# Two token mixers, each with its own order and priorities of parts

## The chip, the core and the metric

The program runs on one core of a Trainium2 chip. The metric is the device time of one execution in microseconds, as a median over runs. The engines are named as the profile names them: PE (TensorE, matrix products; PEld is its weight load), DVE (VectorE), ACT (ScalarE), POOL (GpSimd) and SP (SyncE, which here only issues transfers).

## The reference, cut to what matters

Two layers work on 256 tokens of 1024 features, in float32:

```
x = x + 0.5 * swiglu(rms_norm(x), ...)               # first half step
proj = rms_norm(x) @ w_in                            # RWKV | attention | gates
o_a = rwkv7_mixer(...)      # two scans (forward, backward), 8 heads of 64
o_b = diff_attention(...)   # 4 heads, two softmax maps each
x = x + (sigmoid(g_A) * (o_a @ P_A) + sigmoid(g_B) * (o_b @ P_B)) @ w_out
x = x + 0.5 * swiglu(rms_norm(x), ...)               # second half step
```

The scan multiplies a 64 x 64 state of each head by a decay, corrects it by a rank-one term and adds an outer product for every token. It is the part that can't be written as one large product.

## The kernel before, in words

Activations lie with features in partitions. A large product runs in three float32r passes over a split of both operands in a high and a low part. So a weight tile of 128 x 1024 goes through `weights` (L129): SP issues its load (`wr`, L133), ACT rounds it (`wh`, L135), DVE subtracts to get the rest (`wl`, L139), and PE multiplies (L145 to L147, 24 products of 256 columns for a tile of a projection; L643 to L645, 12 of 512 columns, for attention).

The scan is done in chunks of 64 tokens. Two heads make a pair, and there are four pairs. The parts of a mixer, by the names that the plan uses, are:

- `rw`: low-rank decay and rate parts (three projected tiles). `k0` to `k3`: key and receptance of a pair (two tiles each, `shifted`, L227, whose DVE step on the finished bank is L233). `v0`, `v1`: values of two pairs (two tiles each).
- `w0` to `w3`: a pair of heads (`pair_front`, `unit_front`, `unit_back`). `unit_back` multiplies into PSUM banks of the pool `back` (L331, L337), and DVE empties them under masks (L409, L410, L416, L418 or L421). The last `unit_back` of a pair is held until the next `rwkv_rest`; `x0` and `x1` call it for pairs 1 and 3.
- `i0`, `i1` (`invert`, L435): inverses of the 32 x 32 diagonal blocks of pairs 0, 1 and of pairs 2, 3. The blocks go through DRAM so that one lies in each partition, and then DVE does 22 products (L458) and 22 sums (L459), each of which needs the one before. The first are of a few elements, the last of 1024. POOL multiplies the blocks by a mask meanwhile (L452). The scratch `tv` has one buffer, so `i1` runs after `i0`.
- `m0`, `m1` (`merge_blocks`): the blocks off the diagonal. `c0`, `c1` (`chain`): the scan over four chunks for two pairs each; `c1` also does the group norms (last DVE step L607).
- `at`: twelve weight tiles of attention and the norms of queries and keys (L655 to L663). `ac`: attention itself, head by head; its last steps give `ob`, which shows as icl (L718, L719).
- `g1`, `g0`: eight gate tiles for each branch. `B`: the first branch's product, of `ob`. Behind the plan come branch A, the output product and the next half step.

What runs when is set by a planner at compile time. It simulates the program and hands out, on each engine, the instruction that is ready and comes first by number; the number is the place in the text, and `high_priority(n)` takes n places off it (a negative n adds places). So an instruction further back in the plan fills in where those before it aren't ready. `@` (`issue_after`) queues a part's PE instructions behind the last PE instruction of another part. Tiles of one tag are given out in the order of the text, whatever the numbers are: three places for `wr` and `wh`, two for `wl`, two each for the banks `gen` and `back`, one for `att`. The queue of each engine is fixed then, and the chip runs it in order.

Before, both layers use one string (L37) and one table of priorities (L40):

```
PLAN = "rw k0 w0 k1 w1 x0 i0 k2 w2 v0 k3 w3 v1@w1 x1 i1 m0 c0 m1 c1 at ac@w0 g1@k3 g0@m1 B@w2"
PR = {'k3': -150, 'B': 60}
```

Of the kernel before, what the change touches and what calls it, by code (L numbers as in the profile page):

```python
"""Hybrid bidirectional encoder trunk: macaron SwiGLU halves around RWKV-7 and differential attention.

Activations stay feature-major on chip ([feature in partition, feature tile, token]); weights stream
once. Float32 products of the large matrices are carried by float32r passes over an exact split of
both operands into a high and a low part.
"""
# [11 lines left out]
F32 = mybir.dt.float32  # L18
F32R = mybir.dt.float32r
AF = mybir.ActivationFunctionType  # L20
ALU = mybir.AluOpType
# [3 lines left out]
P = 128  # L25
# [11 lines left out]
PLAN = "rw k0 w0 k1 w1 x0 i0 k2 w2 v0 k3 w3 v1@w1 x1 i1 m0 c0 m1 c1 at ac@w0 g1@k3 g0@m1 B@w2"  # L37
T3 = 0
GATE = {}
PR = {'k3': -150, 'B': 60}  # L40
# [5 lines left out]
# tiles that share a place with others  # L46
PLACE = {"b0": "ar0", "b1": "ar1", "b2": "wt0", "b3": "wt1", "b4": "ab", "b5": "qb", "ak2": "x"}

# columns of the packed vectors
# [5 lines left out]
class Trunk:  # L55
# [21 lines left out]
    def slot(self, tag, shape, dt=F32, half=False):  # L77
        """A tile of 8 KB (or 4) in a partition; tiles of one tag follow each other in place."""
        tag, n = PLACE.get(tag, tag), int(np.prod(shape[1:]))
        t = self.sp.tile([P, 1024 if half else 2048], dt, tag=tag, name=self.nm(tag))  # L80
        v = t[:, :n]
        names = "abcd"[:len(shape) - 1]
        if len(names) > 1:
            v = v.rearrange(f"p ({' '.join(names)}) -> p {' '.join(names)}", **dict(zip(names, shape[1:])))
        return v
# [42 lines left out]
    # weights ------------------------------------------------------------------------------------  # L128
# [56 lines left out]
    # feed-forward half step ---------------------------------------------------------------------  # L185
# [32 lines left out]
    # one tile of x @ W for two feature tiles, in a bank -----------------------------------------  # L218
# [8 lines left out]
    def shifted(self, l, tiles, outs):  # L227
        """outs = p + mu * (centred_shift(p) - p) of RWKV column tiles."""
# [86 lines left out]
    def rwkv_pair(self, p):  # L315
        """A pair of heads in both directions; the last part of the second direction waits for the next call."""
# [16 lines left out]
    def turn(self, out, a):  # L333
        """out[h] = a[h].T for both halves of the partitions."""
# [25 lines left out]
    def unit_front(self, p, d, st, sig, a2, da):  # L360
# [3 lines left out]
        # 2 * iclr - 1 = tanh of half the logit  # L364
# [32 lines left out]
    def unit_back(self, p, d, st, bw, kw):  # L397
# [26 lines left out]
        if d == 1:  # L424
            # sum over a head of r * r_k * (k of both directions)
# [8 lines left out]
    # (I - A)^-1 of the 32 x 32 diagonal blocks, one in a partition ---------------------------------  # L434
    def invert(self, q):  # L435
# [25 lines left out]
        # 16 x 16 blocks, row by row from below: X[i, j:] = G[i, j:] X[j:, j:]  # L461
# [7 lines left out]
        # the block off the diagonal: X01 = X00 G01 X11, with X00 G01 in the place below G's diagonal  # L469
# [19 lines left out]
    def merge_blocks(self, q):  # L489
        """The blocks off the diagonal: T = D + D A D."""  # L490
# [17 lines left out]
    # the scans, chunk by chunk --------------------------------------------------------------------  # L508
    def chain(self, l, q):
        """Two pairs of heads, both directions: the forward scan at chunk j, the other at chunk 3 - j."""  # L510
# [98 lines left out]
    # differential attention -----------------------------------------------------------------------  # L609
# [19 lines left out]
    def attention(self, l):  # L629
        nc, io, vec = self.nc, self.io, self.vec[l]  # L630
        mm = nc.tensor.matmul
        qkt = self.qkt = self.slot("icl", [P, 2, 4, S])
        va = self.va = self.slot("va", [P, 2, 512], half=True)
        for i in range(3):
            ps = [self.acc(), self.acc()]
            for c in range(4):
                wh, wl = self.weights(io["watt"][l, i, :, c * CW:(c + 1) * CW], CW)
                for b in range(2):
                    k = 2 * c + b
                    h, w = wh[:, b * 512:(b + 1) * 512], wl[:, b * 512:(b + 1) * 512]  # L640
                    for t in range(2):
                        ts = slice(t * P, (t + 1) * P)
                        mm(ps[t], self.xh[:, k, ts], h, start=k == 0, stop=False)  # L643
                        mm(ps[t], self.xl[:, k, ts], h, start=False, stop=False)
                        mm(ps[t], self.xh[:, k, ts], w, start=False, stop=k == KD - 1)  # L645
            for t in range(2):
                sc = self.rsT[:, t:t + 1]
                if i == 2:
                    nc.scalar.activation(va[:, t], ps[t], AF.Copy, scale=sc)
                    continue  # L650
                q, sq = [self.f2().rearrange("p a (b c) -> p (a b) c", c=64) for _ in range(2)]
                nc.scalar.activation(q, ps[t].rearrange("p (a b) -> p a b", a=8), AF.Copy, scale=sc)
                nc.scalar.activation(sq, q, AF.Square)
                ms, rq = self.tmp("n8", [P, 8], bufs=4), self.tmp("n8", [P, 8], bufs=4)
                nc.vector.tensor_reduce(ms, sq, AX.X, ALU.add)  # L655
                nc.vector.tensor_scalar(ms, ms, 1.0 / 64, EPS, ALU.mult, ALU.add)
                nc.gpsimd.tensor_tensor(rq, ms, self.mhalf[:, 0:8], ALU.pow)
                nc.vector.tensor_tensor(q, q, rq.unsqueeze(2).to_broadcast([P, 8, 64]), ALU.mult)
                pt = self.att()
                qf = q.rearrange("p a b -> p (a b)")  # L660
                for h in range(4):
                    nc.tensor.transpose(pt[:, h * P:(h + 1) * P], qf[:, h * P:(h + 1) * P], self.ident)
                nc.scalar.activation(qkt[:, i, :, t * P:(t + 1) * P], pt.rearrange("p (a b) -> p a b", a=4), AF.Copy,  # L663
                                     scale=vec[:, V_QG + i:V_QG + i + 1])

    def attention_core(self, l):
# [3 lines left out]
        for h in range(4):  # L670
# [17 lines left out]
            # e0 / s0 - lambda * e1 / s1 = (e0 - lambda * s0 / s1 * e1) / s0  # L688
# [32 lines left out]
    # the token mixer ------------------------------------------------------------------------------  # L721
    def gates(self, l, b):
        """2 * sigmoid - 1 = tanh of half the logits, kept in DRAM until the branch is ready; a step a feature tile."""
# [197 lines left out]
```

## Time and profile before

| | |
|---|---|
| Median of three runs (lowest, highest) | 1406.25 us (1405.81, 1408.23) |
| Profiled execution, first to last instruction | 1406.5 us |
| PE busy | 1349.9 us (96%) |
| PEld busy | 1285.0 us (91%) |
| DVE busy | 940.7 us (67%) |
| ACT busy | 664.8 us (47%) |
| POOL busy | 288.2 us (20%) |

The page gives no other time of the profiled execution than its span, which is 0.3 us above the median of the runs. PE is busy nearly throughout, so what an order can change is the time in which PE waits. The half steps have next to none. The two mixers lie at about 217 to 515 us and 910 to 1210 us, and the slices of the page in which PE drops below its usual share are theirs.

### The profile page before, as it was taken

The numbers are of one execution on the slowest core, as the hardware profiler recorded it, in microseconds if no ns is written. First come the engines' busy times: TensorE is split into PE (matmuls) and PEld (weight loads), VectorE is DVE, ScalarE is ACT, GpSimd is POOL, SyncE is SP. The second block draws the span as 40 slices with busy tenths as digits, with TensorE's granted clock in tenths as the row PEclk, the third lists the DMA queues.
The fourth block names the chain that finished last, engine by engine and source line by source line (L and its number), as shares of the span: only waits on it lengthen the run. The fifth ranks groups of instructions, "written<-read, shape, count | busy, mean of one in ns | idle before, by whom it ended". The sixth has DMA issues, their size and how long they took to land.

```text
span 1406.5 us, 30996 instructions
## 1 busy us (share of the span) xinstructions
PE 1349.9 (96%) x12916; PEld 1285.0 (91%) x12916; DVE 940.7 (67%) x1421; ACT 664.8 (47%) x1059; POOL 288.2 (20%) x284
## 2 busy tenths in 40 slices
PE   6999999998989999999999999999988999999999
PEld 6999998877889899999999999988767888999998
DVE  4655557799957766555556655588999577656644
ACT  5444445344444455444444444554543554544432
POOL 3111015445001112111111111154540010211100
PEclk9999999999999999999999999999999999999999
DMA  6555664325333565556655556633352445555564
GB/s 230 182 181 182 180 207 156 99 91 138 108 103 116 191 229 177 185 181 179 181 184 187 183 174 183 218 111 113 93 143 83 114 136 193 175 187 184 183 188 143
DMA packets 90333, 227.60 MB, mean 162 GB/s; under 512 B 29264, under 2 KB 35408, under 8 KB 89680
## 3 DMA queue, kind: packets, MB, share of 16 engines
q1 hardware_dynamic: 78640, 207.16, 47.0%
q10 hardware_dynamic: 11552, 18.46, 3.9%
q8 instruction: 101, 1.65, 0.5%
q14 instruction: 40, 0.33, 0.1%
HBM read 214.05 MB, written 11.53 MB: 160 GB/s over the span
## 4 chain that ended last, share of the span: by engine, by line
PE 80%; DVE 11%; DMA 3%; issue 2%; ACT 2%; POOL 2%; ACTq 0%; SPq 0%; DVEq 0%; POOLq 0%
PE acc L147 23%; PE acc L146 23%; PE acc L145 23%; DVE tv L458 3%; DVE wl L139 3%; DVE lora L459 2%; PE back L331 1%; PE gen L331 1%; PE att L679 1%; PE back L337 1%; PE gen L283 1%; DMA x<-xd 1%; DMA x<-x 1%; DMA f<-g 0%; PE acc L643 0%
## 5 line engine op out<-in xcount | busy, mean ns | idle before, releaser
L135 ACT ACTIVATE wh<-wr 128x1024 fp32r<-128x1024 f32 (+1 forms) x390 | 404.9, 1039 | 414.7 <-PE acc L146 268.6
L139 DVE TENSOR_TENSOR wl<-wr,wh 128x1024 fp32r<-128x1024 f32 (+1 forms) x390 | 475.5, 1219 | 171.0 <-PE acc L147 83.0
L145 PE MATMUL acc<-xh,wh 128*128 128x256 f32 x1904 | 540.2, 286 | 11.8 <-ACT wh L135 11.8
L146 PE MATMUL acc<-xl,wh 128*128 128x256 f32 x1904 | 539.5, 285 | 0.0
L147 PE MATMUL acc<-xh,wl 128*128 128x256 f32 x1904 | 529.9, 286 | 2.4 <-DVE wl L139 2.1
L145 PEld LDWEIGHTS acc<-xh,wh 128*128 128x128 f32 x1904 | 367.0, 193 | 17.3 <-ACT wh L135 12.0
L146 PEld LDWEIGHTS acc<-xl,wh 128*128 128x128 f32 x1904 | 367.0, 193 | 3.2 <-issue 2.5
L147 PEld LDWEIGHTS acc<-xh,wl 128*128 128x128 f32 x1904 | 360.6, 193 | 9.4 <-issue 3.5
L204 POOL TENSOR_TENSOR t<-t,t 128x256 f32<-128x256 f32 x88 | 89.3, 1016 | 403.7 <-ACT t L202 403.7
L145 PE MATMUL acc<-ar,wh 128*128 128x256 f32 x512 | 144.9, 283 | 0.0
L147 PE MATMUL acc<-ar,wl 128*128 128x256 f32 x512 | 144.9, 283 | 0.0
L199 DVE TENSOR_TENSOR t<-acc,rs 128x512 f32<-128x512 f32 x88 | 60.8, 692 | 119.7 <-PE acc L147 114.6
L146 PE MATMUL acc<-wt,wh 128*128 128x256 f32 x384 | 108.9, 284 | 0.0
L145 PEld LDWEIGHTS acc<-ar,wh 128*128 128x128 f32 x512 | 98.3, 192 | 0.0
L147 PEld LDWEIGHTS acc<-ar,wl 128*128 128x128 f32 x512 | 98.3, 192 | 0.0
L145 PE MATMUL acc<-wt,wh 128*128 128x256 f32 x320 | 91.0, 286 | 3.4 <-DVE x L839 2.2
L166 POOL TENSOR_TENSOR vv<-vv,t 128x256 f32<-128x256 f32 x42 | 36.8, 876 | 279.4 <-ACT t L165 271.8
L147 PE MATMUL acc<-wt,wl 128*128 128x256 f32 x320 | 91.5, 286 | 1.3 <-DVE wl L139 1.2
L458 DVE TENSOR_TENSOR tv<-lora 64x8 f32<-64x8 f32 (+10 forms) x88 | 74.9, 852 | 1.9
L146 PEld LDWEIGHTS acc<-wt,wh 128*128 128x128 f32 x384 | 74.4, 194 | 0.0
L146 PE MATMUL acc<-ab,wh 128*128 128x256 f32 x256 | 72.4, 283 | 0.0
L145 PEld LDWEIGHTS acc<-wt,wh 128*128 128x128 f32 x320 | 61.9, 194 | 4.0 <-issue 2.4
(234 smaller groups left out, 1935.1 us busy)
## 6 DMA issues: line engine op xcount, KB each, us to landing
wr<-f1i SPq DMA_DIRECT2D x88, 512.0 KB, 3.7
wr<-f2i SPq DMA_DIRECT2D x88, 512.0 KB, 3.6
wr<-win SPq DMA_DIRECT2D x62, 512.0 KB, 3.6
wr<-f1o SPq DMA_DIRECT2D x32, 512.0 KB, 3.6
wr<-f2o SPq DMA_DIRECT2D x32, 512.0 KB, 3.6
wr<-watt SPq DMA_DIRECT2D x24, 512.0 KB, 3.7
wr<-wbr SPq DMA_DIRECT2D x16, 512.0 KB, 3.6
wr<-wout SPq DMA_DIRECT2D x16, 512.0 KB, 3.4
```

Source lines behind the costliest of these rows:

```text
L135: nc.scalar.activation(wh[:, :n], raw[:, :n], AF.Copy)
L139: nc.vector.tensor_tensor(wl[:, :n], raw[:, :n], wh[:, :n].bitcast(F32), ALU.subtract)
L145: mm(out, wh, xh, start=first, stop=False)
L146: mm(out, wh, xl, start=False, stop=False)
L147: mm(out, wl, xh, start=False, stop=last)
L166: nc.gpsimd.tensor_tensor(self.sq, self.sq, sq, ALU.add)
L199: nc.vector.tensor_tensor(gu, ps.rearrange("p (a b) -> p a b", a=2), self.rs.unsqueeze(1).to_broadcast([P, 2, S]), ALU.mult)
L204: nc.gpsimd.tensor_tensor(h, s, gu[:, 1], ALU.mult)
L283: mm(ps, dw[r, t * P:(t + 1) * P], w2[r], start=True, stop=True)
L331: self.nc.tensor.matmul(out[r], a[r], b[r], start=start, stop=stop)
L458: mul = lambda o, a, b: ops.append(nc.vector.tensor_tensor(o, a, b, ALU.mult).ins)
L459: add = lambda o, a: ops.append(nc.vector.tensor_reduce(o, a, AX.X, ALU.add).ins)
```

## The change

One plan and one table of priorities become two of each, chosen by the layer. In the first layer `i0` and `i1` come behind all four pairs (`k2 k3 w2 v0 w3 x1 i0 v1 i1`), `c1` comes behind `at` and `ac`, `B` loses its `@w2`, and `w0` and `v1` get numbers 150 places lower and `k2` 200 higher. The second layer keeps the old order; `w2` gets `@w0`, and `g0` and `c1` get numbers 300 and 100 places higher. `attention` and `gates` can be called in pieces now, but both plans call them whole (`at` loops over the three pieces in place).

```diff
-PLAN = "rw k0 w0 k1 w1 x0 i0 k2 w2 v0 k3 w3 v1@w1 x1 i1 m0 c0 m1 c1 at ac@w0 g1@k3 g0@m1 B@w2"
+PLANS = (
+    "rw k0 w0 k1 w1 x0 k2 k3 w2 v0 w3 x1 i0 v1@w1 i1 m0 c0 m1 at ac@w0 c1 g1@k3 g0@m1 B",
+    "rw k0 w0 k1 w1 x0 i0 k2 w2@w0 v0 k3 w3 v1@w1 x1 i1 m0 c0 m1 c1 at ac@w0 g1@k3 g0@m1 B@w2",
+)
...
-PR = {'k3': -150, 'B': 60}
+PRS = ({'k3': -150, 'B': 60, 'v1': 150, 'k2': -200, 'w0': 150},
+       {'k3': -150, 'B': 60, 'g0': -300, 'c1': -100})
...
-    def attention(self, l):
+    def attention(self, l, i):
...
         elif f == "at":
-            self.attention(l)
+            for i in range(3):
+                self.attention(l, i)
...
-        for f in PLAN.split():
+        for f in PLANS[l].split():
             f, *after = f.split("@")
...
-                with self.tc.high_priority(PR[f]) if PR.get(f) else nullcontext():
+                with self.tc.high_priority(PRS[l][f]) if PRS[l].get(f) else nullcontext():
                     self.part(l, f)
```

## Rows read from the trace of the kernel before

**Rows 1.** The page: its first line, and DVE's split of the weights.

```profile
span 1406.5 us, 30996 instructions
...
L139 DVE TENSOR_TENSOR wl<-wr,wh 128x1024 fp32r<-128x1024 f32 (+1 forms) x390 | 475.5, 1219 | 171.0 <-PE acc L147 83.0
```

**Rows 2.** Stretches of both mixers: length, busy time by engine, granted clock, DMA.

```profile
core 0: us, PE busy (x) PEld busy (x) DVE busy (x) ACT busy (x) POOL busy (x), PEclk, DMA share, GB/s
217.00:280.00 63.00, 62.61 (x624) 54.51 (x624) 50.53 (x92) 32.84 (x58) 33.61 (x37) 1.00 0.36 113
280.00:343.30 63.30, 57.95 (x529) 46.52 (x528) 61.72 (x119) 27.15 (x48) 32.84 (x23) 0.95 0.36 110
343.30:394.00 50.70, 44.45 (x569) 39.40 (x569) 47.97 (x74) 24.30 (x40) 0.62 (x1) 0.87 0.43 122
394.00:466.00 72.00, 68.61 (x1079) 62.35 (x1075) 46.67 (x99) 35.92 (x84) 6.83 (x8) 0.99 0.40 122
...
973.00:1040.00 67.00, 59.73 (x546) 47.82 (x544) 63.84 (x116) 30.11 (x50) 39.02 (x23) 0.97 0.38 114
```

**Rows 3.** Timeline of PE, 294 to 333 us: where it waited (start, us, idle before).

```profile
298.67 1.15 PE L337 MATMUL back<-ident,t 64*64 64x64 f32 x32 [1.55 <-DVE qb L410]
301.69 0.40 PE L331 MATMUL back<-ar,t 64*64 64x128 f32 x2 [1.41 <-DVE n L656]
...
327.80 1.15 PE L337 MATMUL back<-ident,t 64*64 64x64 f32 x32 [1.11 <-DVE n L656]
330.26 1.97 PE L331 MATMUL back<-ar,t 64*64 64x128 f32 x16 [1.19 <-DVE qk L418]
```

**Rows 4.** Timeline of DVE ahead of the first two waits.

```profile
296.60 0.74 DVE L458 TENSOR_TENSOR tv<-lora 64x338 f32<-64x338 f32 x1
...
297.79 0.41 DVE L409 TENSOR_TENSOR ab<-back,masks 128x256 f32<-128x256 f32 x1
298.12 0.41 DVE L410 TENSOR_TENSOR qb<-back,masks 128x256 f32<-128x256 f32 x1
...
301.14 0.41 DVE L418 TENSOR_TENSOR qk<-back,masks 128x256 f32<-128x256 f32 x1
```

**Rows 5.** Stretches, the inversions' products (L458) alone: length, DVE busy, clock, DMA.

```profile
280.00:343.30 63.30, 20.78 (x22) 0.95 0.36 110
343.30:391.00 47.70, 16.95 (x22) 0.90 0.43 123
```

**Rows 6.** The same stretches, the inversions' sums (L459) alone.

```profile
280.00:343.30 63.30, 11.60 (x22) 0.95 0.36 110
343.30:391.00 47.70, 11.20 (x22) 0.90 0.43 123
```

**Rows 7.** Timelines of DVE: largest product of each inversion, and the last sum.

```profile
337.17 4.25 DVE L458 TENSOR_TENSOR tv<-lora 64x1024 f32<-64x1024 f32 x1
...
387.03 1.88 DVE L458 TENSOR_TENSOR tv<-lora 64x1024 f32<-64x1024 f32 x1
...
389.40 1.22 DVE L459 TENSOR_REDUCE lora<-tv 64x64 f32<-64x1024 f32 x1
```

**Rows 8.** Timeline of POOL beside the first inversion.

```profile
312.40 0.74 POOL L385 TENSOR_TENSOR t<-t,kr 128x256 f32<-128x256 f32 x1 [4.06 <-ACT t L377]
314.93 4.59 POOL L384 TENSOR_TENSOR ar<-kr,e 128x256 f32<-128x256 f32 x1 [1.79 <-ACT e L375]
...
337.09 2.39 POOL L452 TENSOR_TENSOR ab<-ab,masks 128x1024 f32<-128x1024 f32 x1 [3.06 <-DMA d<-ab]
```

**Rows 9.** Timelines of PE and DVE at the first mixer's end: attention's and the scan's last.

```profile
465.37 0.62 PE L145 MATMUL acc<-icl,wh 128*128 128x256 f32 x3 [0.78 <-ACT icl L718]
...
479.30 0.42 DVE L607 TENSOR_TENSOR x<-t,x 128x256 fp32r<-128x256 f32 x1
```

**Rows 10.** Timeline of DVE: the last of the eight L233 steps of the first mixer.

```profile
281.76 0.67 DVE L233 TENSOR_TENSOR t<-acc,rs 128x512 f32<-128x512 f32 x1
```

**Rows 11.** Timeline of SP's queue: the last gate weights, the first of branch B.

```profile
427.28 7.31 SPq L133 DMA_DIRECT2D wr<-win  x2
440.69 0.33 SPq L133 DMA_DIRECT2D wr<-wbr  x1
```

More of the change, by code (lines that the diff above doesn't have):

```diff
@@ L627, in lambdas @@
         nc.vector.tensor_scalar(sg, vec[:, V_SG:V_SG + 1], 1.0 - lam_init, None, ALU.mult)
-    def attention(self, l):
+    def attention(self, l, i):
         nc, io, vec = self.nc, self.io, self.vec[l]
         mm = nc.tensor.matmul
[L632 to L664, printed above, removed]
@@ new lines, in attention @@
+        if self.qkt is None:
+            self.qkt = self.slot("icl", [P, 2, 4, S])
+            self.va = self.slot("va", [P, 2, 512], half=True)
+        qkt, va = self.qkt, self.va
+        ps = [self.acc(), self.acc()]
+        for c in range(4):
+            wh, wl = self.weights(io["watt"][l, i, :, c * CW:(c + 1) * CW], CW)
+            for b in range(2):
+                k = 2 * c + b
+                h, w = wh[:, b * 512:(b + 1) * 512], wl[:, b * 512:(b + 1) * 512]
+                for t in range(2):
+                    ts = slice(t * P, (t + 1) * P)
+                    mm(ps[t], self.xh[:, k, ts], h, start=k == 0, stop=False)
+                    mm(ps[t], self.xl[:, k, ts], h, start=False, stop=False)
+                    mm(ps[t], self.xh[:, k, ts], w, start=False, stop=k == KD - 1)
@@ new lines, in attention @@
+        for t in range(2):
+            sc = self.rsT[:, t:t + 1]
+            if i == 2:
+                nc.scalar.activation(va[:, t], ps[t], AF.Copy, scale=sc)
+                continue
+            q, sq = [self.f2().rearrange("p a (b c) -> p (a b) c", c=64) for _ in range(2)]
+            nc.scalar.activation(q, ps[t].rearrange("p (a b) -> p a b", a=8), AF.Copy, scale=sc)
+            nc.scalar.activation(sq, q, AF.Square)
+            ms, rq = self.tmp("n8", [P, 8], bufs=4), self.tmp("n8", [P, 8], bufs=4)
+            nc.vector.tensor_reduce(ms, sq, AX.X, ALU.add)
+            nc.vector.tensor_scalar(ms, ms, 1.0 / 64, EPS, ALU.mult, ALU.add)
+            nc.gpsimd.tensor_tensor(rq, ms, self.mhalf[:, 0:8], ALU.pow)
+            nc.vector.tensor_tensor(q, q, rq.unsqueeze(2).to_broadcast([P, 8, 64]), ALU.mult)
+            pt = self.att()
+            qf = q.rearrange("p a b -> p (a b)")
+            for h in range(4):
+                nc.tensor.transpose(pt[:, h * P:(h + 1) * P], qf[:, h * P:(h + 1) * P], self.ident)
+            nc.scalar.activation(qkt[:, i, :, t * P:(t + 1) * P], pt.rearrange("p (a b) -> p a b", a=4), AF.Copy,
+                                 scale=vec[:, V_QG + i:V_QG + i + 1])
@@ L719, in attention_core, with gates @@
             nc.vector.scalar_tensor_tensor(ob[:, 1, :, ts], p4, sg, ob[:, 0, :, ts].bitcast(F32), ALU.mult, ALU.subtract)
-    def gates(self, l, b):
+    def gates(self, l, b, tiles):
         nc = self.nc
-        gd = self.gd[b] = self.dp.tile([4, P, 2, S], F32, tag=f"g{b}", name=self.nm(f"g{b}"))
-        for j in range(KD):
+        if b not in self.gd:
+            self.gd[b] = self.dp.tile([4, P, 2, S], F32, tag=f"g{b}", name=self.nm(f"g{b}"))
+        gd = self.gd[b]
+        for j in tiles:
             ps = self.project(self.io["win"][l], [15 + 8 * b + j])
@@ L794, in part @@
         elif f == "at":
-            self.attention(l)
+            for i in range(3):
+                self.attention(l, i)
+        elif f in ("a0", "a1", "a2"):
+            self.attention(l, int(f[1]))
         elif f == "ac":
@@ L798, in part @@
         elif f[0] == "g":
-            for _ in self.gates(l, int(f[1])):
+            tiles = {"": range(8), "a": range(4), "b": range(4, 8)}[f[2:]]
+            for _ in self.gates(l, int(f[1]), tiles):
                 pass
@@ L810, in mix @@
         self.lambdas(l)
-        self.gd = {}
+        self.gd, self.qkt = {}, None
         marks = {}
-        for f in PLAN.split():
+        for f in PLANS[l].split():
             f, *after = f.split("@")
```

## The prediction

> **What bounds the kernel now.** I read the page first: a span of 1406.5 us [rows 1], with PE busy for 96% of it. A kernel whose PE is that busy gets faster by an order only where PE waits, so the next view was busy time by stretch [rows 2], where the reader should subtract PE's busy time from the length. In the first mixer PE waits 0.39 us from 217 to 280 (the first two pairs of heads), 5.35 from 280 to 343.3 (pairs 2 and 3 beside inversion 0), 6.25 from 343.3 to 394 (inversion 1) and 3.39 from 394 to 466 (second scan, attention, gates). That is 15.4 us in all, and the most that an order can win here apart from the clock. In the second mixer the stretch beside inversion 0 costs 7.27. The column beside it tells why: DVE is busy for 61.72 of 63.30 us and then for 47.97 of 50.70. Between 280 and 394 DVE is the bound, and PE takes what DVE leaves. The granted clock is 0.95 and 0.87 of full there, against 1.00 before; a clock short by 5% and 13% is worth up to 3.2 and 6.6 us.
>
> Then PE's own waits in the stretch of pairs 2 and 3 [rows 3]: four of them, 1.55, 1.41, 1.11 and 1.19 us, together 5.26 of the 5.35. All stand before products into a bank of `back`, that is, before `unit_back`. DVE's queue at the first shows what held them [rows 4]: an inversion product of 0.74 us starts at 296.60, and only after it and its sum, at 297.79, come the masked copies L409 and L410 that free the bank. `i0` comes before `w2` and `w3` in the plan, so its steps win where both are ready. The two waits put down to L656, an attention norm, stand before products that don't read that tile; the masked copies (as L418 at 301.14) are what they need.
>
> **The parts of the change, costed.** All against the profiled execution, 1406.5 us, which is 0.3 above the median of the runs.
>
> (a) *Pairs 2 and 3 ahead of inversion 0.* Their masked copies now beat the inversion's steps. Two of the waits name a masked copy (1.55 + 1.19 = 2.74), so that is one end; the other is all four, 5.26. I take three quarters, -3.9, since the stretch of pairs 0 and 1, the same work with no inversion beside it, has nearly no wait (0.39, rows 2).
>
> (b) *Inversion 0 slips.* It can start when it did (its blocks come from pairs 0 and 1) and fills in, but steps that used to win now come behind the pairs and stand alone with the fillers, as inversion 1 does. Price of standing alone: 6.25 us of PE wait for inversion 1's 16.95 + 11.20 = 28.15 us of steps [rows 2, 5, 6], 0.22 a us. How much slips: DVE's 61.72 us hold 20.78 + 11.60 = 32.38 us of inversion and ten weight splits at 1.22 [rows 1, 2, 5, 6], which leaves 17.1 us for the pairs, the projections' ends and the attention norms. I take half of it, 8.6 us, as displaced (the other half runs where a pair waits for PE or ACT anyway): +1.9, between 0 and +3.8.
>
> (c) *DVE and POOL collide less.* Both inversions do the same 44 steps, yet the first takes 32.38 us and the second 28.15 [rows 5, 6]. The products make up 3.83 of the 4.23. POOL is busy for 32.84 us beside the first and 0.62 beside the second [rows 2]. The largest product takes 4.25 us at 337.17, while POOL's mask product runs from 337.09 to 339.48, and 1.88 at 387.03, with POOL idle [rows 7, 8]. The same goes the other way: a POOL product of a pair took 4.59 us where its neighbour of the same shape took 0.74 [rows 8]. With the pairs done, fewer of the long steps meet POOL; inversion 1's mask product and the attention norms remain. DVE is the bound, so what it saves shortens the stretch: half, -2.1, between 0 and -4.2.
>
> [...]
>
> (d) *`c1` behind `at` and `ac`.* `at` is over by then, so this only lets attention's steps beat the scan's. Now attention ends last: PE waits 0.78 us for its result at 465.37, while the scan's last norm step ends at 479.72, hidden under branch B [rows 9]. With attention earlier, B covers more of the scan's tail; with the scan later, branch A waits. No row shows the swapped order. I bound it by the stretch's whole wait on both sides, -3.4 to +3.4 [rows 2], and take 0: the two ends are equally near.
>
> (e) *`w0`, `v1`, `k2`, the weights' order k2 k3 v0 v1, `B` without `@w2`.* These reorder projections, and the last of eight projections ends at 281.76 [rows 10], when the inversion has just begun. PE, full until 280, hides them: 0, with 0.4 to gain at most (the wait of that stretch) and one late weight split, 1.2 [rows 1], to lose where that cover is gone. `B` comes behind `w2` anyway.
>
> (f) *The second mixer.* `c1` moves back 100 places, past part of `at`, which has long ended when `c1` can start. `g0` moves back 300 places, behind `B`, but weight tiles are given out in the order of the text: `B` has a number low enough to pass the last gate tile today and its weights still load behind it [rows 11]. `w2@w0` asks for an order that holds. So 0; since the two mixers with one plan differ by 7.27 - 5.35 = 1.9 us in one stretch, I bound a reshuffle by 1.9 either way.
>
> New waits: the only one added is `w2@w0`. Queued behind inversion 0 now are inversion 1 (one `tv`), its loads and stores on SP, `m1`, and through `@m1` all of `g0`. On SP the store and loads of the blocks move behind the four projections' weights, which were issued earlier anyway; on POOL the mask product moves behind the pairs' products, whose delay (4.59 against 0.74) shrinks.
>
> Sum: -3.9 + 1.9 - 2.1 = -4.1, so 1402.4 us.
>
> **The rivals.** A measurement of this kernel can tell about 0.2%, 2.8 us, from no change.
>
> *No change, about 1406.* DVE has the same work between 280 and 394 and is full in both orders, so inversion 1 ends when it did; PE gets its waits back later, as in the stretch of inversion 1 (+3.9 in place of +1.9, and no saving in (c)). This would also come out if most of the new numbers do nothing, as I hold for (e) and (f). For it: 97% busy DVE. Against: the collisions, which are DVE time that an order can save.
>
> *Slower, about 1411.* One mechanism: the end of inversion 1. It ends at 390.6 now [rows 7] and releases `m1`, then `c1` and, by `@m1`, the eight `g0` tiles. If inversion 0 slips by the 8.6 us of (b) and DVE doesn't use the time for work that shortens the rest, `c1` starts 8.6 us later, and of that only (a)'s 3.9 us are PE work done earlier: +4.7, 1411; with all 17.1 us slipping, 1406.5 + 17.1 - 3.9 = 1419.7. It decides where the fillers run dry: once `at` and `g1` are done, nothing but attention's head-by-head chain fills PE before `m1`. For it: one `tv` and 4.25 us steps at the end. Against: the planner fills every gap of DVE, and the tail is full of PE work that can move forward.
>
> *More gain, about 1397.* Pairs and inversion stop colliding: all of (a) and (c), 5.26 + 4.23, and half of the clock's 3.2 us in that stretch, less (b): -9.2. For it: the size of the POOL delay, and a clock that is short only in stretches with waits. [...] Against: the planner still fills in, so they keep meeting.
>
> **How the numbers follow.** Forecast 0.40, no change 0.23, slower 0.22, more gain 0.15. The forecast's own range lets each of its three terms go halfway to its ends: (a) -3.3 to -4.6, (b) +2.9 to +1.0, (c) -1.1 to -3.2, in sum -1.5 to -6.8, so 1399.7 to 1405.0. The full range, 1396 to 1413, takes in the centres of all four cases and leaves out the far ends of the last two, some 0.15. Faster by over 0.2% (below 1403.7) is the forecast and the larger gain, less 0.05 for the outer edge of the forecast that falls short of 2.8 us: 0.50. Within 0.2%: 0.23 and that 0.05, 0.28. Slower: 0.22.
>
> **What the profile after would show.** (a): between the second projections and the start of the bare inversion, no waits of over 1 us before `back`, and the masked copies ahead of inversion steps of the same time. (b): inversion 0 ending later than pairs 2 and 3, both inversions back to back with PE waiting about 0.2 us for each us of steps. (c): inversion 0's 44 steps at about 30 us instead of 32.4. (d): attention's result before the scan's last step. (f): the second mixer in its old order, with the same 300 us within 2. I am wrong if inversion 1 ends later than about 390 us by more than PE's waits shrink, or if the second mixer changes by more than a few us.

## The result and the profile after

The changed kernel took 1416.43 us in the median of 4 runs (1415.99 to 1418.03), beside 1407.24 for the kernel before. The ratio is 1.0067, with a 95% interval of 1.005 to 1.0084: slower by some 9 us, where 1402.4 was forecast and the range ended at 1413. The profiled execution took 1415.99 us, so its rows stand for the median. Its span is 1414.2 us, 1.8 less than its time. So the profile before, with its span of 1406.5, is of the run that took 1408.23, not of one 0.3 us above the median, and the forecast of 1402.4, which counts from that span, means a run of some 1404, still 12 us below the result.

Both mixers got longer. A mixer ends with eight steps on VectorE that add the output product to `x`, the last of them some 2.9 us apart. Here are the seventh of the first mixer and the sixth of the second, before and then after; where this text speaks of a mixer's end, it means the end of these two steps, in every kernel:

```profile
514.63 0.42 DVE L839 SCALAR_TENSOR_TENSOR x<-acc,x 128x256 f32<-128x256 f32 x1 [0.82 <-PE acc L147]
1206.72 0.42 DVE L839 SCALAR_TENSOR_TENSOR x<-acc,x 128x256 f32<-128x256 f32 x1 [0.93 <-PE acc L147]
```

```profile
517.35 0.42 DVE L851 SCALAR_TENSOR_TENSOR x<-acc,x 128x256 f32<-128x256 f32 x1 [0.93 <-PE acc L151]
1214.38 0.42 DVE L851 SCALAR_TENSOR_TENSOR x<-acc,x 128x256 f32<-128x256 f32 x1 [0.93 <-PE acc L151]
```

The first mixer ends at 517.8 in place of 515.1, thus 2.7 us late. The second ends 7.7 us late, so 4.9 arose behind the first, in a mixer that I had priced at zero. (The eighth steps, at 517.9 and 1212.9 before and 520.7 and 1220.6 after, give the same.) All lines of the changed kernel stand 4 to 12 lines further down than their counterparts of before (the inversion's products are L462, its sums L463, the scores' first step L686).

The stretches after, in the columns of [rows 2], whose lines they answer to; the last three are the second mixer's, moved by 2.7 us:

```profile
217.00:280.00 63.00, 61.61 (x624) 54.00 (x623) 50.97 (x94) 32.51 (x57) 31.01 (x37) 1.00 0.36 112
280.00:343.30 63.30, 55.30 (x515) 43.81 (x514) 59.33 (x117) 27.75 (x48) 41.96 (x24) 0.95 0.36 104
343.30:394.00 50.70, 42.77 (x562) 37.87 (x561) 48.70 (x72) 19.86 (x35) 1.45 (x2) 0.93 0.39 110
394.00:466.00 72.00, 69.35 (x1044) 62.42 (x1040) 44.49 (x96) 36.97 (x86) 7.62 (x7) 1.00 0.43 124
975.70:1042.70 67.00, 60.16 (x542) 48.02 (x541) 62.29 (x115) 28.07 (x48) 33.62 (x22) 0.95 0.36 109
1042.70:1092.70 50.00, 43.99 (x556) 39.08 (x554) 45.11 (x74) 20.75 (x37) 3.42 (x3) 0.90 0.40 109
1092.70:1161.70 69.00, 66.08 (x1014) 60.17 (x1014) 42.66 (x89) 34.89 (x79) 5.88 (x7) 0.95 0.38 111
```

The second mixer before, the two stretches that follow the one in [rows 2]:

```profile
1040.00:1090.00 50.00, 42.20 (x594) 37.40 (x595) 47.39 (x76) 21.02 (x38) 0.67 (x2) 1.00 0.38 108
1090.00:1159.00 69.00, 64.14 (x1035) 57.98 (x1033) 45.36 (x98) 35.69 (x84) 6.82 (x8) 1.00 0.42 128
```

Subtract PE's busy time from the length, as before. In the first mixer PE now waits 1.39, 8.00, 7.93 and 2.65 us, where [rows 2] give 0.39, 5.35, 6.25 and 3.39: 4.6 us more, and it is in the stretches of the pairs and the inversions that the waits grew. POOL's column shows the other surprise, 41.96 us beside pairs 2 and 3 instead of 32.84. In the second mixer the picture is another: PE waits less beside inversion 1 (6.01 us against 7.80), yet gets through fewer products (556 against 594), and the granted clock is 0.90 and 0.95 where it was 1.00. An estimate from these rows says how much that is: the length of a stretch times what its clock lacks of full is 11.8 us in the second mixer's three stretches, where it was 2.0, while PE's waits there fall from 19.9 to 15.8 us. By this estimate the second mixer lost its time by the clock in this execution, not by waits.

**The 8.00 us.** PE's waits in that stretch after, by its timeline, but for three of under 0.5 us elsewhere; the counterparts are [rows 3]:

```profile
294.94 1.09 PE L335 MATMUL back<-ar,t 64*64 64x128 f32 x16 [1.08 <-DVE scal L392]
296.54 1.09 PE L335 MATMUL back<-ar,t 64*64 64x128 f32 x16 [0.52 <-DVE t L398]
...
324.62 1.09 PE L335 MATMUL back<-ar,t 64*64 64x128 f32 x16 [0.38 <-DVE t L398]
331.09 1.09 PE L335 MATMUL back<-ar,t 64*64 64x128 f32 x16 [1.54 <-DVE qk L422]
335.54 0.26 PE L434 MATMUL gen<-vec,t 64*64 64x1 f32 x1 [3.35 <-POOL t L396]
```

The waits before a `back` bank, four with 5.26 us in all, are still four but 3.52 us now. A new one of 3.35 us more than takes that back. It stands ahead of L434, the small products that come behind pair 3's second direction. It is put down to a POOL product, L396. POOL's groups in 280 to 343.3, first before, then after (columns: busy us, mean ns):

```profile
L392 POOL TENSOR_TENSOR t<-t,t 128x256 f32<-128x256 f32 x2 | 1.9, 940 | 0.1
L391 POOL TENSOR_TENSOR t<-t,kr 128x256 f32<-128x256 f32 x2 | 1.8, 892 | 0.0
L422 POOL TENSOR_TENSOR qk<-qk,t 128x256 f32<-128x256 f32 x2 | 1.5, 737 | 2.7 <-DVE t L421 2.7
```

```profile
L426 POOL TENSOR_TENSOR qk<-qk,t 128x256 f32<-128x256 f32 x2 | 4.5, 2248 | 3.4 <-DVE t L425 3.4
L395 POOL TENSOR_TENSOR t<-t,kr 128x256 f32<-128x256 f32 x2 | 4.0, 1984 | 0.0
L396 POOL TENSOR_TENSOR t<-t,t 128x256 f32<-128x256 f32 x2 | 3.5, 1733 | 0.2
```

The same six products of the pairs cost 5.2 us before and 12.0 after. (They are three of the four groups of the pairs that grew by some 1.6 us or more. Inversion 0's mask product now reaches into the stretch as well, and the attention norms fell by 1.6 us.) VectorE had its side of it: the inversion's steps did get shorter (22 products, then 22 sums, in 280 to 347.2), 30.89 us against 32.38 in [rows 5, 6]:

```profile
280.00:347.20 67.20, 19.93 (x22) 0.95 0.36 102
```

```profile
280.00:347.20 67.20, 10.96 (x22) 0.95 0.36 102
```

VectorE's steps took 1.5 us less, POOL's six products 6.8 us more. Both hold beyond one execution: in five of the kernels below the first mixer's queues are those of before, in five those of after up to pair 3 (in one of them but for a swap). The inversion's steps take 31.9 to 33.9 us in the former and 30.5 to 31.5 in the latter, POOL's products of the pairs in 280 to 343.3 (all six lines of them) 17.0 to 20.5 and 23.0 to 27.9.

**Inversion 0 starts late.** Timelines of VectorE before, then after: pair 1's last masked copy into `ab`, and the inversion's first step.

```profile
270.76 0.41 DVE L409 TENSOR_TENSOR ab<-back,masks 128x256 f32<-128x256 f32 x1
...
280.66 0.16 DVE L463 COPY lora<-lora 64x2 f32<-64x2 f32 x1 [1.28 <-DMA lora<-d]
```

```profile
272.68 0.41 DVE L413 TENSOR_TENSOR ab<-back,masks 128x256 f32<-128x256 f32 x1
...
283.72 0.16 DVE L467 COPY lora<-lora 64x2 f32<-64x2 f32 x1 [1.49 <-DMA lora<-d]
```

The copy is 1.9 us late, the store and load of the blocks follow it, and the inversion begins 3.1 us late. It ends at 347.1 instead of 343.2, inversion 1 then makes up for some of that and ends at 392.2 instead of 390.6. Attention is hit harder. Its first scores, before and then after:

```profile
352.36 0.69 DVE L680 SCALAR_TENSOR_TENSOR f<-att,dist 128x512 f32<-128x512 f32 x1
```

```profile
360.97 0.69 DVE L686 SCALAR_TENSOR_TENSOR f<-att,dist 128x512 f32<-128x512 f32 x1
```

They are 8.6 us late: on PE the scan's first products, which need inversion 0, now stand ahead of them. What became of that shows in attention's last step, before and then after:

```profile
465.35 0.75 DVE L719 SCALAR_TENSOR_TENSOR icl<-att,sg,icl 128x512 fp32r<-128x512 f32 x1 [0.54 <-ACT icl L718]
```

```profile
469.99 0.75 DVE L725 SCALAR_TENSOR_TENSOR icl<-att,sg,icl 128x512 fp32r<-128x512 f32 x1
```

Attention ends 4.6 us late, while the scan's last step begins at 479.3 in both [rows 9]. The mixer's end lies 47 us behind attention's.

### The profile page after: what moved, and what is told of

The parts are those of the page before. It is cut to its first block, busy times and chain, and to the rows that moved or that the text cites. A ratio compares the mean times of both kernels' runs of the same rounds, so it can differ in the third digit from the quotient of the medians.

```text
span 1414.2 us, 30988 instructions
## 1 busy us (share of the span) xinstructions
PE 1355.9 (96%) x12916; PEld 1289.1 (91%) x12916; DVE 937.1 (66%) x1421; ACT 663.1 (47%) x1059; POOL 298.0 (21%) x284
## 4 chain that ended last, share of the span: by engine, by line
PE 77%; DVE 13%; DMA 4%; POOL 2%; issue 2%; ACT 1%; SPq 0%; ACTq 0%; DVEq 0%; POOLq 0%
PE acc L151 23%; PE acc L150 23%; PE acc L149 23%; DVE tv L462 4%; DVE wl L143 3%; DVE lora L463 2%; DMA x<-xd 1%; PE att L685 1%; PE back L335 1%; PE gen L335 1%; DMA d<-ab 1%; PE gen L287 1%; DMA x<-x 1%; DMA lora<-d 0%; POOL t L395 0%
## 5 line engine op out<-in xcount | busy, mean ns | idle before, releaser
L462 DVE TENSOR_TENSOR tv<-lora 64x8 f32<-64x8 f32 (+10 forms) x88 | 73.9, 840 | 1.9
```

What stands on the lines that cost most here:

```text
L462: mul = lambda o, a, b: ops.append(nc.vector.tensor_tensor(o, a, b, ALU.mult).ins)
```

## The experiments

Each kernel is the changed one with other plans and numbers. "First" is when the first mixer ends in the profile (its seventh output step, as above), "second" the time from there to the second mixer's end (its sixth). "Over before" is the difference of medians to the kernel before, run on the same chip beside it.

| kernel | over before, us | ratio, 95% interval | first, us | second, us |
|---|---|---|---|---|
| before | | | 515.1 | 692.0 |
| after | +9.2 | 1.0067 (1.005 to 1.0084) | 517.8 | 697.0 |
| e_l1 | +1.7 | 1.0013 (0.9997 to 1.003) | 517.0 | 691.3 |
| e_l0 | +7.8 | 1.0056 (1.0036 to 1.0076) | 517.1 | 697.4 |
| e_l0_c1 | +11.9 | 1.0083 (1.0061 to 1.0104) | 523.3 | 696.3 |
| e_l0_inv | +21.1 | 1.0147 (1.0122 to 1.0173) | 530.2 | 703.5 |
| e_l0_at | +15.0 | 1.0104 (1.0088 to 1.0119) | 522.6 | 698.6 |
| e_l0_pri | +23.9 | 1.0162 (1.0116 to 1.0207) | 531.5 | 696.6 |
| e_l0_i0early | +8.7 | 1.007 (1.0044 to 1.0097) | 520.4 | 695.5 |
| e_both_at | +21.8 | 1.0163 (1.0117 to 1.0208) | 533.1 | 706.4 |
| e_old_m0 | +6.5 | 1.0043 (1.0019 to 1.0066) | 515.5 | 700.1 |
| e_new_m0 | +10.0 | 1.0068 (1.0041 to 1.0094) | 520.1 | 698.9 |
| e_k2 | +19.5 | 1.0124 (1.0086 to 1.0163) | 531.1 | 693.4 |
| e_l0_plan | +18.2 | 1.0116 (1.0076 to 1.0157) | 531.0 | 702.6 |
| e_old_w3 | -2.3 | 0.9984 (0.9968 to 1.0001) | 515.5 | 695.1 |
| e_old_at | +0.9 | 1.0005 (0.9985 to 1.0024) | 518.9 | 692.6 |
| e_new_c0 | +14.2 | 1.0095 (1.0067 to 1.0123) | 517.6 | 700.0 |

A single profile is good to about 2 us in a mixer: in before, e_l1, e_old_m0, e_old_w3 and e_old_at the first mixer's queues are the same, and "first" lies between 515.1 and 518.9. Some profiled executions lie far from their kernel's median: e_both_at 10.5 us above it, e_l0_plan 6.4, e_l0_inv 4.8 and e_old_w3 4.0, and below it e_new_c0 4.9, e_k2 3.4 and e_l0_pri 3.0. Their "first" and "second" carry that, so of these kernels only the large differences count.

### Which mixer's edit costs

e_l1 undoes the first mixer's edit, e_l0 the second's:

```diff
 # e_l1: the first mixer as before
-PRS = ({'k3': -150, 'B': 60, 'v1': 150, 'k2': -200, 'w0': 150},
+PRS = ({'k3': -150, 'B': 60},
 # e_l0: the second mixer as before
-       {'k3': -150, 'B': 60, 'g0': -300, 'c1': -100})
+       {'k3': -150, 'B': 60})
```

(and the plan of that mixer likewise).

> The first mixer has its old plan and numbers, the second its new ones. In the profiles the second mixer is 4.9 us longer than before (7.7 late at its end, of which 2.7 came with it from the first). Theory A, the second mixer's own numbers cost that (c1 moved back, g0 moved back): 4 to 6 us over before. Theory B, the second mixer's loss comes from the first one's edit, because the planner writes one order for the whole program and the second mixer's queues come out another way when the first mixer ends elsewhere: 0 to 1.5 us over before. In its order this kernel differs from before only behind the last attention step of the second mixer.

> The first mixer has its new plan and numbers, the second its old ones. Theory A (each mixer pays for its own edit): 2 to 4 us over before, all of it at the end of the first mixer. Theory B (the second mixer's queues are upset by the first one's edit): 6 to 9 us over before, with the second mixer 4 to 6 us longer than before although nothing of its plan is changed. The last product of the first mixer should end near 520 in both.

e_l1 is within what can be told from no change, e_l0 shows nearly the whole loss: +7.8 us, with the second mixer 5.4 us longer than before although its plan and its numbers are the old ones. Theory A falls. The second mixer's own edit is as harmless as I had priced it (in the traces, the second mixer's queues in e_l1 are those of before up to attention's last head, at 1133 us on PE, so `w2@w0` changes nothing; the few places moved from there on are left to the numbers of `c1` and `g0`); what lengthens the second mixer is the edit of the first. In the queues of e_l0 the second mixer has the order of before up to the gate tiles beside inversion 1, and another from there on.

### The parts of the first mixer's edit

e_l0_c1 and e_l0_inv, with the second mixer's old plan:

```diff
 # e_l0_c1: new plan and numbers, c1 back ahead of at and ac
-... m0 c0 m1 at ac@w0 c1 g1@k3 g0@m1 B
+... m0 c0 m1 c1 at ac@w0 g1@k3 g0@m1 B
 # e_l0_inv: old plan and numbers, i0 behind the pairs (and x1, which ends pair 3, ahead of v1)
-rw k0 w0 k1 w1 x0 i0 k2 w2 v0 k3 w3 v1@w1 x1 i1 ...
+rw k0 w0 k1 w1 x0 k2 w2 v0 k3 w3 x1 i0 v1@w1 i1 ...
```

> As e_l0, but in the first mixer c1 stands ahead of at and ac again; all the rest of the first mixer's edit stays. If the swap of scan and attention is what costs the first mixer its 2.7 us (attention's result 4.6 us late, branch B's first product at 470.0 in place of 465.4), the first mixer ends near 516.5 to 517.5, as before or earlier. If the loss comes from the end of the inversions (the first ends 3.8 us later, the second 1.6), it ends at 519 to 521 here too.

> As before, but i0 stands behind the pairs in the first mixer's plan, with the old numbers and nothing else moved (k3 behind v0, c1 ahead of at, B@w2). My prediction's sum for this part alone was -4.1 us in the first mixer: pairs' waits -3.9, the inversion's slip +1.9, fewer meetings of DVE and POOL -2.1. If that sum holds and the other parts spoilt it, the first mixer ends at 512 to 515. If the move itself loses (DVE has the same work, the inversion ends later), it ends at 518 to 521.

Putting `c1` back makes it worse (523.3), so the swap is not what costs; within the new plan it spares some 6 us. The move of `i0` (with `x1` ahead of it), for which my sum gave -4.1, costs 15.1 us in the first mixer, in a profile 4.8 us above its median. Both kernels end later than either of their forecasts said (521 at most). Three more parts of the edit, each with the old plan, and the new plan with `i0` where it was:

```diff
 # e_l0_at: old plan, c1 behind at and ac        # e_both_at: the same in both mixers
-... m0 c0 m1 c1 at ac@w0 g1@k3 g0@m1 B@w2
+... m0 c0 m1 at ac@w0 c1 g1@k3 g0@m1 B@w2
 # e_l0_pri: old plan, new numbers in the first mixer
+PRS = ({'k3': -150, 'B': 60, 'v1': 150, 'k2': -200, 'w0': 150},
 # e_l0_i0early: new plan and numbers, i0 back behind x0
+"rw k0 w0 k1 w1 x0 i0 k2 k3 w2 v0 w3 x1 v1@w1 i1 m0 c0 m1 at ac@w0 c1 g1@k3 g0@m1 B"
```

> The old plan and numbers in both mixers, but in the first c1 stands behind at and ac. Theory C: the first mixer ends 47 to 50 us after attention's last result (466.1 before, 470.7 after, 468.7, 474.8 and 479.8 in e_l0, e_l0_c1 and e_l0_inv), and attention is slow where the scan's steps, which come ahead of it by number, fall beside its heads. Then attention's result comes 3 to 6 us earlier than 466.1 and the first mixer ends 2 to 6 us earlier than 515.1. Theory D: the swap gained 6 us between e_l0_c1 and e_l0 only because the inversion was late there; with the inversion in its old place it gains nothing, 514 to 517.

> The old plan in both mixers, with the new numbers of the first (w0 and v1 150 places ahead, k2 200 back). I had priced these at 0. If they are what spared the new plan some 7 us against e_l0_inv, the first mixer ends before 515.1 here, at 509 to 514; if they do nothing by themselves, at 514 to 517; if they hurt, later.

> The new plan and numbers in the first mixer, but with i0 back in its old place behind x0; the second mixer as before. If the move of i0 is what costs, the first mixer ends 2 to 8 us earlier than in e_l0 (517.1), thus at 509 to 515, with attention's result before 466. If the move is neutral and the other parts set the end, 516 to 518.

> The old plan in both mixers with c1 behind at and ac in both. Theory C: 4 to 10 us faster than before over both mixers. Theory D: within 3 us of before. If the second mixer's order is upset by any edit in the first, its own length (692.0 us from the first mixer's end to its own) grows by 4 us or more whatever its plan.

None of the four gains: the first mixer ends at 522.6, 531.5, 520.4 and 533.1. The forecasts of both theories missed, C's gain as well as D's 514 to 517 and "within 3 us", and e_l0_i0early too ended beyond both of its ranges. In e_l0_at attention does end earlier, but the scan ends later. Its timeline of VectorE, attention's last step and the scan's:

```profile
463.76 0.75 DVE L725 SCALAR_TENSOR_TENSOR icl<-att,sg,icl 128x512 fp32r<-128x512 f32 x1
...
487.15 0.43 DVE L611 TENSOR_TENSOR x<-t,x 128x256 fp32r<-128x256 f32 x1 [0.48 <-ACT x L610]
```

Attention gained 1.6 us against 465.35, the scan lost 7.9 against 479.30, and the mixer ends 7.5 us later. In the second mixer of e_both_at it is starker: the same two steps begin at 1176.35 and 1204.55, and the eighth output step ends 40 us behind the scan's and 68 behind attention's (38 and 61 in the first mixer of e_l0_at).

So of theory C only a part is left. In the first mixer of all kernels but one the end fits the later of two chains: it lies some 47 to 50 us behind attention's, where that one decides (47.0 in after, 50.4 in e_l0_inv), and some 35 behind the scan's, where that one does (35.0 in e_l0_at). Before, both are due at once (466.1 + 47 to 50 is 513 to 516, and 479.7 + 35 is 514.7). That would explain why favouring either one costs; it is read from the ends, and no run holds one chain fixed and moves the other. The exception is e_l0_plan, below, 68 and 40 us behind the two. Most of what it lies over 35 is a third thing: PE waits 3.76 us there for the reload of `x` (L845), which took 9.2 us from issue to landing, and 6.2 before.

e_l0_i0early says something on the plan itself: its first mixer's queues are those of e_l0 but for a swap of neighbours here and there, so with `k2` 200 places back the place of `i0` in the text does nothing. Which of the numbers matters:

```diff
 # e_k2: old plan, one number
+PRS = ({'k3': -150, 'B': 60, 'k2': -200},
 # e_l0_plan: new plan, old numbers
+PRS = ({'k3': -150, 'B': 60},
```

> The old plan in both mixers, with k2 200 places back in the first as the only edit; i0 keeps its place in the text. In e_l0_i0early, where i0 had its old place but k2 its new number, inversion 0 still began at 285.2 and the first mixer's queues were those of e_l0 but for one swap. If k2's number is what moves the inversion and costs, inversion 0 begins at 284 to 286 in place of 281.0 and the first mixer ends 3 to 15 us later than 515.1, like the others with the old place of c1. If it is harmless by itself, 514 to 517.

> The new plan in the first mixer with the old numbers, the second as before. e_l0 has the same plan with the new numbers and ends the first mixer at 517.1. If the numbers spare the new plan what the bare move costs (e_l0_inv 530.2), 522 to 530 here; if it is the place of c1 alone that does, 516 to 519.

`k2`'s number alone costs 16.0 us in the first mixer, the new plan with the old numbers 15.9, and the new plan with all the new numbers (e_l0) about 2. The edits don't add up; each repairs what the other breaks. The expectation of a late inversion 0 in e_k2 missed (its first sum ran at 281.83, before at 281.05). Its timeline of VectorE shows where the loss is instead:

```profile
353.88 0.17 DVE L467 COPY lora<-lora 64x2 f32<-64x2 f32 x1 [4.09 <-DMA lora<-d]
```

This is inversion 1's first step, which in before follows inversion 0's last without a gap, at 343.3. Here VectorE waits for its blocks. SP's queue, the store of pairs 2 and 3's blocks, before and then in e_k2:

```profile
334.35 0.33 SPq L440 DMA_DIRECT2D d<-ab  x1
```

```profile
343.22 0.33 SPq L444 DMA_DIRECT2D d<-ab  x1
```

Pair 3 was late by 8.9 us, and its blocks with it. The inversion ends at 403.8 instead of 390.6. A late end of inversion 1 is what my slower rival named; here it comes from the late blocks of pair 3, not from a slip of inversion 0, and in a kernel that isn't the one predicted.

### Order or carry-over

The second mixer's loss could be its order, or something that the first mixer's edit leaves behind on the chip. With `m0` 60 places back in the second mixer, the planner writes the same queues for it behind either of two first mixers, and that makes a pair:

```diff
 # e_old_m0: the first mixer as before; e_new_m0: the first mixer as after; in both:
-       {'k3': -150, 'B': 60, 'g0': -300, 'c1': -100})
+       {'k3': -150, 'B': 60, 'm0': -60})
```

> First half of a pair. The first mixer's queues are those of before; the second keeps the old plan but m0 gets a number 60 places higher there, which gives its queues an order in which nothing of the first mixer's edit shows. If any other order of the second mixer than that of before costs some 5 us (theory B in its general form: before's order was one good draw), the second mixer takes 695 to 699 from the first one's end in place of 692.0 and the median is 3 to 8 us over before. If only what the first mixer's edit does to it costs, 690 to 694 and within 3 us of before.

> Second half of the pair: the first mixer's queues are those of after, the second mixer's are, instruction by instruction, those of e_old_m0. What is left between the two is the first mixer's edit alone. Theory B (the second mixer's loss is its order): its length is that of e_old_m0 within 2 us, and the medians differ by the first mixer's own loss, 2 to 4 us. Theory E (something that the first mixer's edit carries over on the chip, not in the order, slows the second one): the second mixer is 3 to 6 us longer than in e_old_m0 and the medians differ by 6 to 9.

The same two steps as above, in e_old_m0 and then in e_new_m0:

```profile
515.04 0.42 DVE L851 SCALAR_TENSOR_TENSOR x<-acc,x 128x256 f32<-128x256 f32 x1 [0.60 <-PE acc L151]
1215.19 0.42 DVE L851 SCALAR_TENSOR_TENSOR x<-acc,x 128x256 f32<-128x256 f32 x1 [0.93 <-PE acc L151]
```

```profile
519.72 0.42 DVE L851 SCALAR_TENSOR_TENSOR x<-acc,x 128x256 f32<-128x256 f32 x1 [0.93 <-PE acc L151]
1218.62 0.42 DVE L851 SCALAR_TENSOR_TENSOR x<-acc,x 128x256 f32<-128x256 f32 x1 [0.93 <-PE acc L151]
```

Subtract: 700.15 and 698.90 us. With the same queues the second mixer takes the same time to 1.3 us, and not 3 to 6 us more behind the changed first mixer, so theory E falls. The medians differ by 3.5 us, which is the price of the first mixer's edit alone (from 10 and 5 runs, some 1 to 7 us at 95%). By subtraction some 4 of e_l0's 7.8 us are left for the second mixer's new order. That an order alone can cost as much, e_old_m0 shows directly: 6.5 us over before, with the first mixer's queues of before.

Where the second mixer's time goes shows in its rows as a whole, before, then in e_old_m0 and in e_new_m0 (columns of [rows 2]):

```profile
892.00:1207.10 315.10, 291.51 (x3297) 259.62 (x3296) 250.50 (x442) 148.54 (x269) 86.40 (x78) 0.98 0.43 134
892.40:1215.60 323.20, 301.70 (x3298) 267.32 (x3297) 247.81 (x442) 149.14 (x269) 86.48 (x78) 0.95 0.43 130
897.00:1219.00 322.00, 295.01 (x3298) 261.68 (x3297) 248.98 (x442) 149.16 (x269) 82.29 (x78) 0.97 0.44 131
```

PE waits 23.6, 21.5 and 27.0 us, and the estimate for the clock (length times what it lacks) is about 6, 16 and 10 us: together 30, 38 and 37. What is left of the length is 285 us in all three. So against before, and by this estimate, one and the same queue lost its time by the clock alone in one execution and by clock and waits alike in the other; only the sum is common to both.

### How narrow the old order is

```diff
 # e_old_w3: the second mixer with 'w3': -60; e_old_at: with 'at': 60; the first as before
 # e_new_c0: e_new_m0 with 'c0': -60 in the first mixer
```

> The first mixer's queues are those of before; in the second w3 gets a number 60 places higher, which only swaps some products of attention's projection with pair 3's beside the first inversion, and three steps on VectorE. Theory F (swaps that move neither the inversions' end nor attention's start are free): the second mixer takes 690 to 694 from the first one's end, within 3 us of before. Theory G (before is a narrow optimum, any swap costs): 695 to 699, 3 to 8 us over before.

> The first mixer's queues are those of before; in the second at gets a number 60 places lower, which moves 18 products of one gate tile behind those of attention's projection and swaps a few steps on VectorE at the start of the second inversion. Theory F: 690 to 694 for the second mixer. Theory G: 695 to 699.

> As e_new_m0 in the second mixer, instruction by instruction; the first mixer has its new plan and numbers, with c0 60 places further back, so that attention's third head goes ahead of the first scan's last chunks. If the first scan standing ahead of attention is what costs the first mixer its rest (520.1 in e_new_m0 against 515.5 in e_old_m0, attention's result at 471.5 against 466.4), attention's result comes 2 to 5 us earlier than 471.5 and the first mixer ends at 515 to 518. If it is not, 519 to 522. The second mixer's length should be 698.9 within 2 in either case, since its order is the same.

e_old_w3 and e_old_at take the time of before (-2.3 and +0.9 us in the median; the profile of e_old_w3 alone, 695.1, would have said otherwise). These two local swaps are free and theory G falls; no kernel here is faster than before by more than can be told. e_new_c0 falls on the other side: its median is no better than e_new_m0's (14.2 over before against 10.0), attention's result came only 1.4 us earlier (470.1 against 471.5), though "first" is 517.6 in a profile 4.9 us below its median. So the third head's place isn't the rest of the first mixer's loss.

Its profile shows something else. In after, e_l0, e_new_m0 and e_new_c0 the first mixer's queues are the same up to pair 3, in e_l0_i0early but for one swap, yet the chip runs them in two ways. POOL in after, then in e_l0:

```profile
329.76 2.92 POOL L395 TENSOR_TENSOR t<-t,kr 128x256 f32<-128x256 f32 x1
332.76 2.73 POOL L396 TENSOR_TENSOR t<-t,t 128x256 f32<-128x256 f32 x1
```

```profile
329.70 0.72 POOL L395 TENSOR_TENSOR t<-t,kr 128x256 f32<-128x256 f32 x1
330.50 0.96 POOL L396 TENSOR_TENSOR t<-t,t 128x256 f32<-128x256 f32 x1
```

In after, e_new_m0 and e_l0_i0early both products are long (2.92 and 2.73 us in each) and PE waits 3.35 or 3.36 us at L434; in e_l0 and e_new_c0 they are short (0.72 or 0.73, and 0.96), and the wait is gone, though the one before it grows from some 1.6 to 2.73. PE's waits in 280 to 343.3 are 8.00, 7.75 and 7.89 us in the former and 6.92 and 6.36 in the latter, some 1 to 1.5 us less. "First" (517.8, 520.1 and 520.4 against 517.1 and 517.6) points the same way, but can't show so little. While L396 runs in after, VectorE runs three steps back to back:

```profile
332.95 0.67 DVE L664 TENSOR_TENSOR f<-f,n 128x512 f32<-128x512 f32 x1
333.55 0.41 DVE L398 TENSOR_TENSOR t<-t,e 128x256 f32<-128x256 f32 x1
333.88 1.00 DVE L462 TENSOR_TENSOR tv<-lora 64x512 f32<-64x512 f32 x1
```

L396 takes 2.73 us there, 1.77 more than the 0.96 of e_l0, and the three steps fill 332.95 to 334.88, 1.93 us. The rows show the two engines side by side and the product longer; that the steps hold it up is my reading of them.

In e_l0 it is VectorE whose steps are long. The inversion's product just ahead of pair 3's copies, in after and then in e_l0:

```profile
329.38 0.57 DVE L462 TENSOR_TENSOR tv<-lora 64x256 f32<-64x256 f32 x1
```

```profile
329.85 1.01 DVE L462 TENSOR_TENSOR tv<-lora 64x256 f32<-64x256 f32 x1
```

L386 before it and L387 behind it took 0.92 and 0.94 us there instead of 0.41 each. So the copy L422 began at 332.00 instead of 330.54, and PE, which needs it, waits 2.73 us instead of 1.54. PE waits for a long step in both executions; they differ in whose step it is, POOL's or VectorE's.

## Why the prediction was wrong

The sum had -4.1 us for the first mixer and 0 for the second; in the profile it is +2.7 and +4.9. These are the steps that failed, term by term.

**(a), -3.9: a part of it, and then lost.** The waits before `back` shrank by 1.7 us, but PE's wait in 280 to 343.3 as a whole grew by 2.65. The failed step is "the stretch of pairs 0 and 1 ... has nearly no wait". It is no model of pairs 2 and 3 ahead of the inversion, since the inversion still fills in between their steps, and a pair needs POOL as well as VectorE's masked copies. The 3.35 us behind L396 is nearly twice what the four waits saved, and even where L396 takes 0.96 us (e_l0, e_new_c0) PE waits 6.92 and 6.36 us in that stretch, not less than 5.35.

**(b), +1.9: right in size by luck.** The waits beside inversion 1 grew by 1.7 us, but by another path. Inversion 0 didn't stand alone; it began 3.1 us late, because pair 1's last masked copy came late. "It can start when it did" failed.

**(c), -2.1: VectorE's part right, what it was worth wrong.** I foresaw the inversion's steps at about 30 us, and they took 30.89. But I had the delay of the pairs' POOL products shrink ("4.59 against 0.74") and put nothing on its growing, while the six products named above went from 5.2 to 12.0 us. PE's longest new wait, 3.35 us, stands behind one of these.

**(d), 0 within 3.4: wrong both ways.** In the profiles the swap costs 7.5 us by itself and spares 6.2 within the new plan, both beyond my bounds. "The two ends are equally near" was the right observation with the wrong conclusion: in a tie, moving either end can cost; it doesn't follow that nothing does.

**(e), 0: wrong.** "PE, full until 280, hides them" looked at the projections alone. `k2` 200 places back makes pair 3 and with it inversion 1 late, 16.0 us by itself, and the other parts of the edit take most of it back. That neither the cost nor the repair shows in the sum of single edits is the reason why pricing them one by one could not work here.

**(f), 0 within 1.9: wrong, and over half of the loss.** The second mixer's own edit is worth +1.7, with an interval that includes none. But I priced that edit alone and expected "the second mixer in its old order", while the planner writes one program: the first mixer's edit redraws the second's queues (e_l0: 5.4 us longer with its old plan), and e_old_m0 shows that an order alone costs. In the profile after, the time went in granted clock (by the estimate above, 11.8 us against 2.0), which no term of the sum holds.

Of the rivals, "slower" named the wrong mechanism: inversion 1 ended 1.6 us late, not 8.6. That a late inversion 1 costs is real in e_k2 (13.2 us late there). The two signs that I gave for being wrong were the right ones to watch: the second mixer changed by more than a few us, and PE's waits did not shrink.

What stays open: which of the swaps in the second mixer costs, why one and the same queue loses more by the clock in one execution and more by waits in another, and what is left of the first mixer's 3.5 us (the pair's price) where POOL's two products are short.

## What to carry to other kernels

Where a planner hands out one order for a whole program, an edit to one part can be an edit to every part behind it: diff the queues before pricing anything at zero, and hold the rest of the order fixed (as in the pair) to price the edit alone. When two chains end a stage within a few us, an order can only be judged by the later of the two, and prices of single edits need not add. The order before was such a tie, by the reading above; whether tuned orders in general are, no run here shows.

## What the runs showed of the hardware

**One queue, two ways to run it.** The pair of POOL products took 0.72 and 0.96 us or 2.92 and 2.73 us in kernels with the same queues there, as shown above; where POOL's products were short (e_l0), three VectorE steps of the same stretch took 0.92, 1.01 and 0.94 us instead of 0.41, 0.57 and 0.41.

**The clock.** Products of a gate tile right behind a PE wait, before (behind waits of 2.01 and 0.78 us) and after (1.90 and 0.51):

```profile
1089.49 0.28 PE L145 MATMUL acc<-xh,wh 128*128 128x256 f32 x1
1089.61 0.29 PE L146 MATMUL acc<-xl,wh 128*128 128x256 f32 x1
```

```profile
1096.53 0.42 PE L149 MATMUL acc<-xh,wh 128*128 128x256 f32 x1
1096.74 0.41 PE L150 MATMUL acc<-xl,wh 128*128 128x256 f32 x1
```

The starts are 0.12 us apart before and 0.21 after, for the same shape and after waits that are no longer. In the 10 us around these rows the granted clock is 1.00 before and 0.75 after:

```profile
1082.00:1092.00 10.00, 7.21 (x90) 6.60 (x88) 8.99 (x11) 4.38 (x9) 0.00 (x0) 1.00 0.42 106
```

```profile
1088.00:1098.00 10.00, 7.59 (x69) 6.93 (x66) 9.11 (x12) 4.29 (x7) 0.00 (x0) 0.75 0.40 105
```

**Spread.** The kernel before ran from 1402.8 to 1417.3 us over 63 runs beside these experiments, with a mean clock between 0.979 and 0.994, so that effects of 3 us needed medians, and one profile per kernel did not do.
